# High and low weight parts interleaved element by element in one buffer of a two-layer encoder

## The chip, the cores and the metric

The kernel runs on one core of one Trainium2 chip. The metric is the device time of one execution in microseconds; a lower time is better. All times before come from two timed runs and one execution taken by the hardware profiler.

## The reference

A bidirectional encoder of two layers, 256 tokens, width 2048, all in float32:

```python
def reference(x, ...):
    for i in range(DEPTH):                      # DEPTH = 2
        h = rms_norm(x, attn_norm[i])
        if i % 2 == 0:
            x = x + even_mixer(h, ...)          # 16 heads: 8 neighbourhood, 8 dilated
        else:
            x = x + odd_mixer(h, ...)           # 16 query heads, 4 key/value heads, window 128
        x = x + sq_relu_mlp(rms_norm(x, mlp_norm[i]), w_mlp_in[i], w_mlp_out[i])
    return rms_norm(x, final_norm)

def sq_relu_mlp(h, w1, w2):                     # 2048 -> 8192 -> 2048
    a = jax.nn.relu(h @ w1)
    return (a * a) @ w2
```

Nearly all of the arithmetic is `activation @ weight`: projections into heads, the output projections, and the two large matrices of each MLP. Each weight is used once, for 256 tokens.

## The kernel before

**Precision.** A float32 product is put together from three products in the faster `float32r` format: a value is split into a high part (a copy rounded to `float32r`) and a low part (the value minus its high part), and high × high, high × low and low × high are added up. The activations `u`, `o`, `hid` hold both parts side by side, `[.., 2, 256]`. The weights arrive as plain float32 and are split on the chip, by the function `split(hi, lo, src)`: ScalarE (ACT) writes the high part as a copy (L82), VectorE (DVE) subtracts (L83).

**Tiling.** Weights come in units of 128 output features by 2048 inputs, and a unit in two halves of 8 tiles of 128 × 128 (`HALF = 8`), 512 KB each. `take_half` (from L96) takes the next half off a list written in the order of use, has SyncE (SP) load it into one of six buffers `r` (L100), and splits it into a tile `h` of the pool `whi` and a tile `l` of the pool `wlo`, five buffers each. Rows of these tiles are `ROW = P + 8 = 136` elements apart and 128 of them are used. The list runs two halves ahead of use. For every input tile k, `k_range` (L150 and L152) issues a pair of matmuls into one accumulator: `h` as the stationary operand against both parts of the activation (512 columns), then `l` against the high part (256 columns). In the tables a matmul is one row of PE and its load of the stationary tile one row of PEld.

**Exceptions.** Three things handle weights otherwise. `value_pair` (L272) takes weights as the moving operand and the activations as the stationary one; its halves are marked `flat` and lie without gaps, 1024 elements in a row. Where a unit must be held over a wait, its last two tiles are split into small tiles `hh` and `hl` of the pool `held_w`. And the first three units ("starters", L471 and L473) are loaded in groups of a few tiles together with the input, into tiles allocated at L461; the two halves of three units make six buffers, one more than a pool has.

**Order.** The program is written in the order of PE's use. Attention steps are put into that order some quarter units later (`later`, `tick`), and the framework's scheduler then orders the instructions of each engine by what they depend on and sets the waits. Every engine works its queue in order. A buffer of a pool is written anew when all readers of its last contents are done.

**Names.** `t` and `z` are the evacuation of an accumulator (`joined`, L179 and L181), `hid` the hidden layer's activation, `acc` an accumulator (three of them).

Of the kernel before, what the change touches and what calls it, by code (L numbers as in the profile page):

```python
# [8 lines left out]
F32R = mybir.dt.float32r  # L9
# [5 lines left out]
P = 128  # L15
# [9 lines left out]
SCALE = 128.0 ** -0.5  # L25
TW = 384
HALF = KT // 2
ROW = P + 8
RAW_BUFS = 6
PART_BUFS = 5  # L30

# [10 lines left out]
def encoder(ctx: ExitStack, tc: tile.TileContext, a: dict, outT: bass.AP):  # L42
# [1 line left out]

    const = ctx.enter_context(tc.tile_pool(name="const", bufs=1))
    raw = ctx.enter_context(tc.tile_pool(name="raw", bufs=RAW_BUFS))
    whi = ctx.enter_context(tc.tile_pool(name="whi", bufs=PART_BUFS))
    wlo = ctx.enter_context(tc.tile_pool(name="wlo", bufs=PART_BUFS))
    held_w = ctx.enter_context(tc.tile_pool(name="held_w", bufs=3))
    work = ctx.enter_context(tc.tile_pool(name="work", bufs=3))  # L50
    acc_ps = ctx.enter_context(tc.tile_pool(name="acc_ps", bufs=3, space=PSUM))
# [29 lines left out]
    def split(hi, lo, src):  # L81
        nc.scalar.activation(hi, src, AF.Copy)  # L82
        nc.vector.tensor_sub(lo, src, hi.bitcast(F32))  # L83
# [6 lines left out]
    def need(units, held=0, flat=False):  # L90

        for i, src in enumerate(units):
            pending.extend([(src[:, :HALF, :], HALF, flat),
                            (src[:, HALF:, :], HALF - 2 if i < held else HALF, flat)])

    def take_half():  # L96
        while pending and len(loaded) <= AHEAD:
            src, n, flat = pending.pop(0)
            r = raw.tile([P, HALF, P], F32, name="r")
            nc.sync.dma_start(r, src)  # L100
            h = whi.tile([P, HALF, ROW], F32R, name="h")
            l = wlo.tile([P, HALF, ROW], F32R, name="l")
            if flat:
                h, l = (w.rearrange("p k c -> p (k c)")[:, :HALF * P] for w in (h, l))
                split(h, l, r.rearrange("p k c -> p (k c)"))
                loaded.append((h, l, None))
                continue
            h, l = h[:, :, :P], l[:, :, :P]
            split(h[:, :n, :], l[:, :n, :], r[:, :n, :])
            tiles = [(h[:, k, :], l[:, k, :]) for k in range(n)]  # L110
            if n < HALF:
                h, l = (held_w.tile([P, 2, P], F32R, name=name) for name in ("hh", "hl"))
                split(h, l, r[:, n:, :])
                tiles += [(h[:, k, :], l[:, k, :]) for k in range(2)]
            loaded.append((h, l, tiles))
        return loaded.pop(0)

    def take_unit():
        return take_half()[2] + take_half()[2]
# [65 lines left out]
    def gained(k, which):  # L185
        x, gk = xs[:, k, :], g[:, which, k:k + 1]
        if which == 4:
            nc.scalar.activation(x, x, AF.Copy, scale=gk)
        else:
            nc.scalar.activation(u[:, k, 0, :], x, AF.Copy, scale=gk)  # L190
            nc.vector.scalar_tensor_tensor(u[:, k, 1, :], x, gk, u[:, k, 0, :].bitcast(F32),
                                           op0=ALU.mult, op1=ALU.subtract)
# [68 lines left out]
    def value_pair(pool, keep):  # L261

        ps = acc_ps.tile([P, 2, T], F32, name="acc")
        for half in range(2):
            parts = [take_half()[:2] for _ in range(2)]
            for kk in range(HALF):
                k = half * HALF + kk
                h, l = (w[:, (kk % 4) * T:(kk % 4 + 1) * T] for w in parts[kk // 4])
                for j in range(2):
                    js = slice(j * P, (j + 1) * P)  # L270
                    for n, (x, y) in enumerate(((0, h), (0, l), (1, h))):
                        nc.tensor.matmul(ps[:, j, :], u[:, k, x, js], y,  # L272
                                         start=k == 0 and j == 0 and n == 0,
                                         stop=k == KT - 1 and n == 2, skip_group_check=True)
                if kk % 2 == 1:
                    tick()
        assert norm["ready"]
        w = pool.tile([P, 2, 2, T], F32R, name="v", bufs=1)
        for j in range(2):
            nc.scalar.activation(w[:, 0, j, :], ps[:, j, :], AF.Copy, scale=rcol[:, j:j + 1])  # L280
            nc.vector.scalar_tensor_tensor(w[:, 1, j, :], ps[:, j, :], rcol[:, j:j + 1],
                                           w[:, 0, j, :].bitcast(F32), op0=ALU.mult, op1=ALU.subtract)
        keep.append(w)
# [158 lines left out]
    STARTERS = 3  # L442
# [14 lines left out]
    hl = [None] * STARTERS  # L457
    for k0, k1 in GROUPS:
        ks = slice(k0 % HALF, (k1 - 1) % HALF + 1)
        if k0 % HALF == 0:  # L460
            hl = [(whi.tile([P, HALF, ROW], F32R, name="h")[:, :, :P], wlo.tile([P, HALF, ROW], F32R, name="l")[:, :, :P])  # L461
                  for _ in range(STARTERS)]
        for i in range(STARTERS):
            split(hl[i][0][:, ks, :], hl[i][1][:, ks, :], rs[k0 // HALF][i][:, ks, :])
            if i == 0:
                for k in range(k0, k1):
                    gained(k, 0)
        for i in range(STARTERS):
            h, l = hl[i]
            for k in range(k0, k1):  # L470
                nc.tensor.matmul(sps[i], h[:, k % HALF, :], u[:, k].rearrange("p a t -> p (a t)"),  # L471
                                 start=k == 0, stop=False)
                nc.tensor.matmul(sps[i][:, :T], l[:, k % HALF, :], u[:, k, 0, :], start=False, stop=k == KT - 1)  # L473
# [12 lines left out]
    with tc.tile_pool(name="attn0", bufs=1) as pool:  # L486
# [24 lines left out]
        for p in range(8):  # L511
            q, k, v = [[], []], [[], []], []
            for i in range(2):
# [6 lines left out]
                h = 2 * p + i  # L520
# [11 lines left out]
    with tc.tile_pool(name="attn1", bufs=1) as pool:  # L532
        o = pool.tile([P, NH, 2, T], F32R, name="o")
        sl = slopes(16)
        for p in range(2):
            k, v = [[], []], []
# [8 lines left out]
            for i in range(8):  # L545
                h = 8 * p + i
# [93 lines left out]
```

## Time and profile before

| | |
|---|---|
| median of the timed runs | 2112.02 us (2111.78 to 2112.26, 2 runs) |
| the profiled execution | 2113.29 us, span 2111.4 us |
| PE busy | 2088.1 us, 12,438 matmuls |
| PEld busy | 1846.7 us, 12,438 loads |
| DVE busy | 1339.8 us |
| ACT busy | 1036.6 us |
| split, DVE's part (L83, tiles l) | 729 instructions, 880.6 us |
| split, ACT's part (L82, tiles h) | 729 instructions, 762.8 us |
| DMA | 386.06 MB, mean 183 GB/s |

The stages, in us from the span's start: start to 60; attention of layer 0 to 325; its output projection to 440; MLP of layer 0 to about 1125; then key, value and query projections of layer 1 with attention to 1300 (the table of the prediction cuts at 1195, shortly before the second group of eight heads); output projection to 1400; the second MLP to 2100. Busy times count instructions; matmuls overlap, so the time from one start to the next says how fast PE goes. A releaser is what ended an engine's idle time.

### The profile page before, as it was taken

What the parts mean: (1) busy time and instruction counts of PE and PEld (TensorE: products, weight loads), DVE (VectorE), ACT (ScalarE), POOL (GpSimd) and SP (SyncE); (2) the same over time, 40 slices, a digit from 0 to 9 for tenths busy, and PEclk for the clock granted to TensorE, in tenths of its full rate; (3) what the DMA queues carried; (4) which work ended last, traced back from release to release, by engine and by line L of the source; (5) the groups of instructions that cost most, each with busy time, mean ns of one, the idle gap of its engine ahead of it and who ended that gap; (6) DMA issues with size and microseconds to landing.
All of it is one profiled execution on the core that took longest, in us unless ns stands there. A gap on an engine that the chain in (4) does not pass through costs nothing.

```text
span 2111.4 us, 31825 instructions
## 1 busy us (share of the span) xinstructions
PE 2088.1 (99%) x12438; PEld 1846.7 (87%) x12438; DVE 1339.8 (63%) x2088; ACT 1036.6 (49%) x1602; POOL 23.0 (1%) x33
## 2 busy tenths in 40 slices
PE   8999999999999999999999999999999999999997
PEld 6999998888888888888889998888888888888887
DVE  6766676666655556666656877766665556665554
ACT  6555555544444444444445656554444434444442
POOL 2100000000000000000000000000000000000000
PEclk9999999999999999999999999999999999999999
DMA  9755555555555555555555454555555555555552
GB/s 260 176 174 167 168 174 174 191 185 189 189 188 189 189 189 189 190 189 190 189 189 185 149 163 144 190 185 188 189 189 189 189 189 189 189 189 190 189 189 91
DMA packets 108294, 386.06 MB, mean 183 GB/s; under 512 B 12352, under 2 KB 13392, under 8 KB 108144
## 3 DMA queue, kind: packets, MB, share of 16 engines
q1 hardware_dynamic: 106992, 381.73, 55.1%
q0 software_dynamic: 1008, 2.27, 1.5%
q8 instruction: 97, 1.59, 0.3%
q14 instruction: 53, 0.43, 0.1%
q10 hardware_dynamic: 144, 0.04, 0.0%
HBM read 381.89 MB, written 2.10 MB: 182 GB/s over the span
## 4 chain that ended last, share of the span: by engine, by line
PE 96%; DMA 2%; DVE 1%; ACT 0%; SPq 0%; issue 0%; DVEq 0%; ACTq 0%
PE acc L150 58%; PE acc L152 30%; PE acc L272 5%; PE s_ps L296 1%; PE m_ps L340 1%; DMA r<-in_even_w_in 1%; PE p_ps L321 1%; DMA r<-in_even_w_v 1%; DMA xs<-in_xT 0%; ACT h L82 0%; DVE l L83 0%; DVE xs L570 0%; PE acc L147 0%; PE acc L148 0%; PE m_ps L225 0%
## 5 line engine op out<-in xcount | busy, mean ns | idle before, releaser
L83 DVE TENSOR_TENSOR l<-r,h 128x1024 fp32r<-128x1024 f32 (+3 forms) x729 | 880.6, 1208 | 701.9 <-ACT h L82 699.3
L82 ACT ACTIVATE h<-r 128x1024 fp32r<-128x1024 f32 (+3 forms) x729 | 762.8, 1047 | 966.0 <-PE acc L150 635.9
L150 PE MATMUL acc<-u,h 128*128 128x512 f32 x2820 | 988.4, 394 | 0.0
L152 PE MATMUL acc<-u,l 128*128 128x256 f32 x2820 | 788.6, 280 | 0.0
L150 PE MATMUL acc<-hid,h 128*128 128x512 f32 x2016 | 702.4, 393 | 0.0
L150 PEld LDWEIGHTS acc<-u,h 128*128 128x128 f32 x2820 | 529.9, 188 | 119.2
L152 PE MATMUL acc<-hid,l 128*128 128x256 f32 x2048 | 572.3, 279 | 0.0
L152 PEld LDWEIGHTS acc<-u,l 128*128 128x128 f32 x2820 | 529.1, 188 | 0.2
L150 PEld LDWEIGHTS acc<-hid,h 128*128 128x128 f32 x2016 | 378.7, 188 | 87.3
L152 PEld LDWEIGHTS acc<-hid,l 128*128 128x128 f32 x2048 | 384.1, 188 | 0.0
L150 PE MATMUL acc<-o,h 128*128 128x512 f32 x500 | 175.2, 394 | 1.1 <-DVE z L181 1.1
L152 PE MATMUL acc<-o,l 128*128 128x256 f32 x500 | 139.8, 280 | 0.0
L272 PE MATMUL acc<-h,u 128*128 128x256 f32 x640 | 119.9, 283 | 0.0
L181 DVE TENSOR_TENSOR z<-acc,t 128x256 f32<-128x256 f32 x275 | 114.4, 418 | 2.2 <-ACT t L179 2.1
L150 PEld LDWEIGHTS acc<-o,h 128*128 128x128 f32 x500 | 93.9, 188 | 22.8 <-DVE z L181 1.7
L179 ACT ACTIVATE t<-acc 128x256 f32<-128x256 f32 x275 | 100.8, 367 | 5.5 <-PE acc L152 2.7
L272 PEld LDWEIGHTS acc<-h,u 128*128 128x128 f32 x640 | 101.1, 190 | 0.5
L152 PEld LDWEIGHTS acc<-o,l 128*128 128x128 f32 x500 | 93.8, 188 | 0.0
L272 PE MATMUL acc<-l,u 128*128 128x256 f32 x320 | 90.1, 281 | 0.0
L272 PEld LDWEIGHTS acc<-l,u 128*128 128x128 f32 x320 | 60.9, 190 | 0.1
L382 DVE SCALAR_TENSOR_TENSOR z<-z 128x256 f32<-128x256 f32 x128 | 54.2, 425 | 4.2
L83 DVE TENSOR_TENSOR hid<-z,hid 128x256 fp32r<-128x256 f32 x128 | 53.5, 419 | 1.3 <-ACT hid L82 1.2
(94 smaller groups left out, 857.6 us busy)
## 6 DMA issues: line engine op xcount, KB each, us to landing
r<-in_w_mlp_in SPq DMA_DIRECT2D x256, 512.0 KB, 4.5
r<-in_w_mlp_out SPq DMA_DIRECT2D x256, 512.0 KB, 4.5
r<-in_even_w_in SPq DMA_DIRECT2D x58, 512.0 KB, 4.2
r<-in_odd_w_qkv SPq DMA_DIRECT2D x40, 512.0 KB, 4.0
r<-in_even_w_v SPq DMA_DIRECT2D x32, 512.0 KB, 3.8
r<-in_even_w_out SPq DMA_DIRECT2D x32, 512.0 KB, 4.2
r<-in_odd_w_out SPq DMA_DIRECT2D x32, 512.0 KB, 3.8
r<-in_odd_w_v SPq DMA_DIRECT2D x8, 512.0 KB, 4.1
```

Source lines behind the costliest of these rows:

```text
L82: nc.scalar.activation(hi, src, AF.Copy)
L83: nc.vector.tensor_sub(lo, src, hi.bitcast(F32))
L150: nc.tensor.matmul(ps, h, act[:, k].rearrange("p a t -> p (a t)"), start=start, stop=False)
L152: nc.tensor.matmul(ps[:, :T], l, act[:, k, 0, :], start=False, stop=stop)
L179: nc.scalar.activation(t, ps[:, T:], AF.Copy)
L181: nc.vector.tensor_add(z, ps[:, :T], t)
L272: nc.tensor.matmul(ps[:, j, :], u[:, k, x, js], y, start=k == 0 and j == 0 and n == 0, stop=k == KT - 1 and n == 2, skip_group_check=True)
L296: nc.tensor.matmul(s_ps[:, i, :], qh[:, x, qs], kh[:, y, :], start=n == 0, stop=n == 2)
L321: nc.tensor.transpose(p_ps[:, j, i * P:(i + 1) * P], s[:, i, j * P:(j + 1) * P], ident)
L340: nc.tensor.matmul(o_ps[:, :T], vv[:, x, j, side * P:(side + 1) * P], pt[:, y, j, :], start=n == 0, stop=n == 5)
L382: nc.vector.scalar_tensor_tensor(z, z, 0.0, z, op0=ALU.max, op1=ALU.mult)
```

## The change

The pools `whi` and `wlo` become one pool `parts_w` of five buffers whose rows are `2 * P + 8 = 264` elements apart. High parts lie in the elements 0, 2, 4, ... of a row and low parts in 1, 3, 5, .... ACT therefore writes every other element, DVE reads the high part and writes the low part with the same step, and each load of a stationary tile reads 128 elements at a step of two elements (8 bytes). The small held tiles are interleaved in the same way. The halves of `value_pair` are not: there the high part fills the first 1024 elements and the low part the next 1024. The number and shapes of the instructions stay the same.

```diff
-ROW = P + 8
+ROW = 2 * P + 8
...
-    whi = ctx.enter_context(tc.tile_pool(name="whi", bufs=PART_BUFS))
-    wlo = ctx.enter_context(tc.tile_pool(name="wlo", bufs=PART_BUFS))
+    parts_w = ctx.enter_context(tc.tile_pool(name="parts_w", bufs=PART_BUFS))
...
+    def interleaved(w):
+        return w[:, :, 0:2 * P:2], w[:, :, 1:2 * P:2]
+
     def take_half():
         while pending and len(loaded) <= AHEAD:
             src, n, flat = pending.pop(0)
             r = raw.tile([P, HALF, P], F32, name="r")
             nc.sync.dma_start(r, src)
-            h = whi.tile([P, HALF, ROW], F32R, name="h")
-            l = wlo.tile([P, HALF, ROW], F32R, name="l")
+            w = parts_w.tile([P, HALF, ROW], F32R, name="w")
             if flat:
-                h, l = (w.rearrange("p k c -> p (k c)")[:, :HALF * P] for w in (h, l))
+                w = w.rearrange("p k c -> p (k c)")
+                h, l = w[:, :HALF * P], w[:, HALF * P:2 * HALF * P]
                 split(h, l, r.rearrange("p k c -> p (k c)"))
                 loaded.append((h, l, None))
                 continue
-            h, l = h[:, :, :P], l[:, :, :P]
+            h, l = interleaved(w)
             split(h[:, :n, :], l[:, :n, :], r[:, :n, :])
             tiles = [(h[:, k, :], l[:, k, :]) for k in range(n)]
             if n < HALF:
-                h, l = (held_w.tile([P, 2, P], F32R, name=name) for name in ("hh", "hl"))
+                h, l = interleaved(held_w.tile([P, 2, 2 * P], F32R, name="hw"))
                 split(h, l, r[:, n:, :])
...
         if k0 % HALF == 0:
-            hl = [(whi.tile([P, HALF, ROW], F32R, name="h")[:, :, :P], wlo.tile([P, HALF, ROW], F32R, name="l")[:, :, :P])
-                  for _ in range(STARTERS)]
+            hl = [interleaved(parts_w.tile([P, HALF, ROW], F32R, name="w")) for _ in range(STARTERS)]
```

On PE the order is the same but for a few attention steps, which stand up to ten places earlier or later among the pairs. On ACT and DVE neighbours change places. What moves are waits. The first place is the start, at the sixth starter buffer, the one that no pool has free; ACT's queue before:

```order
L82 ACTIVATE h<-r 128x4x128 [waits DMAHW6_49]
L190 ACTIVATE u<-xs,g 128x256 x2
L82 ACTIVATE h<-r 128x4x128 [waits DMAHW7_49]
L82 ACTIVATE h<-r 128x4x128 [waits DMAHW0_49,PE_49]
L199 ACTIVATE sq<-xs 128x256 [waits DVE_49]
```

The same place of ACT's queue in the changed kernel, where w is the shared tile:

```order
L81 ACTIVATE w<-r 128x4x128 [waits DMAHW6_49]
L192 ACTIVATE u<-xs,g 128x256 x2
L81 ACTIVATE w<-r 128x4x128 [waits DMAHW7_49]
L81 ACTIVATE w<-r 128x4x128 [waits DMAHW0_49,DVE_49,PE_49]
L201 ACTIVATE sq<-xs 128x256 [waits DVE_49]
```

The copy into the sixth buffer now waits for DVE as well, which wrote the low part there, and its wait for PE covers the low part's matmuls too. DVE's queue at the same place, before:

```order
L83 TENSOR_TENSOR l<-r,h 128x4x128 [waits DMAHW6_49,Activation_49]
L191 SCALAR_TENSOR_TENSOR u<-xs,g,u 128x256 [waits Activation_49] x2
L83 TENSOR_TENSOR l<-r,h 128x4x128 [waits DMAHW7_49,Activation_49]
L83 TENSOR_TENSOR l<-r,h 128x4x128 [waits DMAHW0_49,PE_49,Activation_49]
L200 TENSOR_TENSOR ssq<-ssq,sq 128x256 [waits DVE_49,Activation_49]
```

And in the changed kernel:

```order
L82 TENSOR_TENSOR w<-r,w 128x4x128 [waits DMAHW6_49,Activation_49]
L193 SCALAR_TENSOR_TENSOR u<-xs,g,u 128x256 [waits Activation_49] x2
L82 TENSOR_TENSOR w<-r,w 128x4x128 [waits DMAHW7_49,Activation_49]
L82 TENSOR_TENSOR w<-r,w 128x4x128 [waits DMAHW0_49,Activation_49]
L202 TENSOR_TENSOR ssq<-ssq,sq 128x256 [waits DVE_49,Activation_49]
```

DVE's subtraction has lost its wait for PE; it waits for ACT's copy, which has waited for PE. The second place is ACT's queue in the middle of the first MLP's hidden units, before (h a high part, t an evacuation, hid the hidden activation):

```order
L82 ACTIVATE h<-r 128x8x128 [waits DMAHW5_49,PE_49,Activation_49]
L179 ACTIVATE t<-acc 128x256 [waits PE_49,Activation_49]
L82 ACTIVATE h<-r 128x8x128 [waits DMAHW6_49,PE_49]
L82 ACTIVATE hid<-z 128x256 [waits DVE_49]
L82 ACTIVATE h<-r 128x8x128 [waits DMAHW7_49,PE_49,Activation_49]
L179 ACTIVATE t<-acc 128x256 [waits PE_49,Activation_49]
```

And in the changed kernel:

```order
L81 ACTIVATE w<-r 128x8x128 [waits DMAHW0_49,PE_49,Activation_49]
L181 ACTIVATE t<-acc 128x256 [waits PE_49,Activation_49]
L81 ACTIVATE w<-r 128x8x128 [waits DMAHW1_49]
L81 ACTIVATE hid<-z 128x256 [waits DVE_49]
L81 ACTIVATE w<-r 128x8x128 [waits DMAHW2_49,PE_49,Activation_49]
L181 ACTIVATE t<-acc 128x256 [waits PE_49,Activation_49]
```

The order of kinds is the same. Every second copy has no wait for PE of its own any more: its buffer comes free with the last low-part matmul of a unit, for which the evacuation ahead of it has already waited.

## The prediction

> **What bounds the kernel now.** First the page's busy shares, the granted clock and the chain that ended last.
>
> ```profile
> PE 2088.1 (99%) x12438; PEld 1846.7 (87%) x12438; DVE 1339.8 (63%) x2088; ACT 1036.6 (49%) x1602; POOL 23.0 (1%) x33
> ...
> PEclk9999999999999999999999999999999999999999
> ...
> PE 96%; DMA 2%; DVE 1%; ACT 0%; SPq 0%; issue 0%; DVEq 0%; ACTq 0%
> ```
>
> TensorE is busy 99% of the span and makes 96% of the chain. So only two things can move the time: the cadence of the matmuls, or another engine that becomes late enough to stop them. The cadence is read from the timeline of a moment deep in the first MLP.
>
> ```profile
> 1004.56 0.40 PE L150 MATMUL acc<-hid,h 128*128 128x512 f32 x1
> 1004.56 0.19 PEld L152 LDWEIGHTS acc<-hid,l 128*128 128x128 f32 x1
> 1004.80 0.28 PE L152 MATMUL acc<-hid,l 128*128 128x256 f32 x1
> 1004.80 0.19 PEld L150 LDWEIGHTS acc<-hid,h 128*128 128x128 f32 x1
> 1004.91 0.40 PE L150 MATMUL acc<-hid,h 128*128 128x512 f32 x1
> 1004.92 0.19 PEld L152 LDWEIGHTS acc<-hid,l 128*128 128x128 f32 x1
> 1005.15 0.28 PE L152 MATMUL acc<-hid,l 128*128 128x256 f32 x1
> 1005.15 0.19 PEld L150 LDWEIGHTS acc<-hid,h 128*128 128x128 f32 x1
> ```
>
> Starts matter here, not durations, since the instructions overlap. A high-part matmul (512 columns) holds PE from 1004.56 to 1004.80 and a low-part matmul (256 columns) from 1004.80 to 1004.91; the pair comes round every 0.35 us. Each matmul has a weight load of its own, issued when the matmul before it starts. The low part's load has a slot of 0.23 to 0.24 us, the next high part's load only 0.11 to 0.12 us. The load takes 0.19 us from start to end, longer than the short slot, so successive loads overlap, and what is exclusive in a load is shorter than its duration. The groups by shape give the number of pairs, and the chain gives the two slots and a stretch in which every matmul has 256 columns and a load.
>
> ```profile
> L150 PE MATMUL acc<-u,h 128*128 128x512 f32 x2820 | 988.4, 394 | 0.0
> ...
> L150 PE MATMUL acc<-hid,h 128*128 128x512 f32 x2016 | 702.4, 393 | 0.0
> L150 PEld LDWEIGHTS acc<-u,h 128*128 128x128 f32 x2820 | 529.9, 188 | 119.2
> ...
> L150 PE MATMUL acc<-o,h 128*128 128x512 f32 x500 | 175.2, 394 | 1.1 <-DVE z L181 1.1
> ```
> ```profile
> 122.06 0.23 PE acc L150
> 122.28 0.12 PE acc L152
> 122.40 1.42 PE acc L272 x12
> ...
> 124.26 5.66 PE acc L272 x48
> ```
>
> That is 2820 + 2016 + 500 = 5,336 pairs, about 0.348 us each: 1,857 of the 2,111 us. The value projections (L272) run at 5.66 / 48 = 0.118 us a matmul.
>
> **The change part by part.** Base: the profiled execution took 2113.3 us, its span 2111.4 and 1.9 around it; the median of the runs is 2112.0, so the sum is made as a difference and put on the median.
>
> *Matmuls and loads.* None is added or removed; both halves of a pair now load their stationary tile with a step of 8 bytes, 1,024 bytes of a partition instead of 512. The trace of before has no such load. From below: 0, because a load is no limit as long as its exclusive part fits the short slot of 0.117 us. From above: if that part fills the slot already and goes with the bytes it spans, the short slot becomes 0.234 us, and 5,336 × 0.117 = +624 us. I take 0. The row it is nearest to is the moving operand's: the high-part matmul reads 512 contiguous elements, 2,048 bytes of each partition, in 0.23 us, so 1,024 bytes take half of that, 0.115 us. A load that touches 1,024 bytes at that rate still fits 0.117 us, though barely. A value below 0 is weighed with the rivals.
>
> The Trainium skill ("TensorE: Matmul & The Clock Gate", LDWEIGHTS) speaks against this comfort: it gives a load as its columns over 1.2 per ns, an estimate of 107 ns for 128, which would leave 10 ns of the slot. By it any slowing of a load by over a tenth shows, and a doubling costs an estimated 97 ns a pair, +518 us in all. The 117 ns slots do not contradict it.
>
> *Splits.* ACT's copy now writes every other element; DVE reads h and writes l that way.
>
> ```profile
> L83 DVE TENSOR_TENSOR l<-r,h 128x1024 fp32r<-128x1024 f32 x702 | 860.6, 1226 | 688.7 <-ACT h L82 686.2
> L82 ACT ACTIVATE h<-r 128x1024 fp32r<-128x1024 f32 x702 | 744.9, 1061 | 946.6 <-PE acc L150 625.2 <-issue 289.5 <-PE acc L272 11.8
> ...
> L83 DVE TENSOR_TENSOR l<-r,h 128x256 fp32r<-128x256 f32 x6 | 2.5, 424 | 5.8 <-ACT h L82 5.8
> ...
> L82 ACT ACTIVATE h<-r 128x256 fp32r<-128x256 f32 x6 | 2.5, 410 | 5.5 <-DMA r<-in_even_w_in 5.5
> ```
>
> Per element DVE costs (1226 − 424) / 768 = 1.044 ns and ACT (1061 − 410) / 768 = 0.848 ns. No row has a stepped access of these engines, so the bounds are: nothing, and a doubling of the part per element (twice the bytes spanned). That part is 1,069 of DVE's 1,226 ns (87%) and 868 of ACT's 1,061 (82%). Whether PE would feel it is read by stage, all work first and then only the instructions that read the raw tiles, the splits:
>
> ```profile
> 325.00:440.00 115.00, 114.51 (x659) 100.14 (x659) 78.56 (x126) 63.71 (x104) 0.00 (x0) 1.00 0.56 183
> 440.00:1195.00 755.00, 755.00 (x4390) 663.40 (x4389) 467.06 (x668) 355.62 (x508) 0.00 (x0) 1.00 0.57 187
> 1195.00:1300.00 105.00, 104.91 (x694) 95.54 (x693) 82.58 (x206) 63.37 (x138) 0.00 (x0) 1.00 0.46 152
> 1300.00:1400.00 100.00, 99.44 (x575) 87.02 (x574) 69.78 (x111) 57.02 (x94) 0.00 (x0) 1.00 0.56 184
> 1400.00:2085.00 685.00, 685.00 (x3933) 599.79 (x3933) 409.10 (x540) 316.70 (x429) 0.00 (x0) 1.00 0.57 185
> ```
> ```profile
> 325.00:440.00 115.00, 49.52 (x45) 43.16 (x44) 1.00 0.56 183
> 440.00:1195.00 755.00, 329.04 (x273) 284.61 (x271) 1.00 0.57 187
> 1195.00:1300.00 105.00, 36.91 (x33) 32.62 (x34) 1.00 0.46 152
> 1300.00:1400.00 100.00, 43.49 (x39) 37.50 (x38) 1.00 0.56 184
> 1400.00:2085.00 685.00, 300.46 (x248) 261.24 (x246) 1.00 0.57 185
> ```
>
> Columns: in the first table PE, PEld, DVE, ACT, POOL after the length; in the second DVE and ACT. DVE idles 36.4, 287.9, 22.4, 30.2 and 275.9 us in these stages. A doubling adds 87% of the second table: 43.2, 286.9, 32.2, 37.9 and 262.0. It overflows by 6.8, 9.8 and 7.7 us in the first, third and fourth stage and just fits in the two MLP stretches: +24 us. ACT always fits (tightest: 63.4 + 0.82 × 32.6 = 90 of 105 us). So the splits are priced 0 to +24 us; I take 0, because the rows of these engines show times per element, no times per byte.
>
> *Waits.* As the order shows, ACT's copy now waits for the last low-part matmul on the old buffer, and DVE's subtraction no longer waits for PE.
>
> ```profile
> DVE l L83 <- ACT h L82: 699.3, 659, 4.1
> ACT h L82 <- PE acc L150: 635.9, 432, 2.0
> ...
> PEld acc L471 <- ACT h L82: 7.7, 5, 2.2
> ```
>
> The first two rows say that splits are run as soon as a buffer comes free. With five buffers, a freed one is read again four halves later, 4 × 8 × 0.348 = 11.1 us; copy and subtraction take 1.06 + 1.23 = 2.3 us of that. The release comes later by one low-part slot, 0.12 us (0.35 us where the next high part lies between), and behind the waiting copy on ACT stand the evacuation t and the hidden layer's copy; the three accumulators cover those. Without that cover it would be at most 0.35 us a half. Where it bites is the start, the only place where PE's loads waited for splits for long (third row): the sixth starter buffer, +0.4 us at most. If the splits doubled, the start would lose some 3 us, five waits of a 512-element split that is 0.43 to 0.53 us longer. The swaps of neighbours on ACT and DVE cost nothing by the same 11.1 us.
>
> Sum: 2112.0 + 0 + 0 + 0.4 = **2112.4 us**.
>
> **The rivals.** *Slower: the stepped load becomes the bound* (the other side). Place: the short slot. It decides from the point where a load's exclusive part exceeds 0.117 us. In full it gives 2112 + 624 = 2736 us. In part, say 5 to 25 ns over the slot, 5,336 × 5 to 25 ns = +27 to +133 us, 2139 to 2245. For it: there is no more than one short slot for each pair, PE has nothing to hide a longer load behind, and the byte argument leaves 2 ns. Against: the rate of the moving stream.
>
> *DVE becomes the bound.* Up to a doubling 2112 to 2139 us; over 2% slower only from 2.05 times the time per element, where the two MLP stretches overflow as well (at that factor 8.9 + 13.4 + 11.4 + 9.6 = 43 us). At 2.4 times, where I end this case, the same table overflows by 24 + 114 + 23 + 23 + 91 = 275 us: 2387.
> The Trainium skill's "Vector Engine (DVE) Microarchitecture Reference" (5.2, measured stream behaviour) has a rule for this: a port keeps its rate only for runs of two adjacent 4-byte words, which a step of two never gives; its rows run from 1.71 to 2.50 ns a column, and by my stage table that is nothing at 1.75 and an estimated +270 us at 2.50. "SBUF — State Buffer" (its cacheline note) says two hits on a 16-byte line suffice, which a step of 8 bytes gives: nothing. No run here shows either yet.
>
> *Faster: the pair gets shorter.* At half the granted clock (the column after POOL in the second fence) a pair took 0.64 us:
>
> ```profile
> 21.20 0.41 PE L473 MATMUL acc<-u,l 128*128 128x256 f32 x1
> 21.41 0.63 PE L471 MATMUL acc<-u,h 128*128 128x512 f32 x1
> 21.84 0.41 PE L473 MATMUL acc<-u,l 128*128 128x256 f32 x1
> ```
> ```profile
> 21.00:22.50 1.50, 1.50 (x6) 1.21 (x6) 1.50 (x5) 1.23 (x4) 0.00 (x0) 0.50 0.77 78
> ```
>
> Half of that is 0.320, so 0.028 us a pair is lost at full clock. If the stationary reads from two buffers caused it and one buffer removed it, 5,336 × 0.028 = −149 us, 1963 us. Against: L272, whose stationary tile lies in u, loses as much (0.118 where half the clock's 0.21 gives 0.107).
>
> That the step would not reach PE is excluded: in the order both matmuls of a pair take the one tile w, with unchanged shapes.
>
> **How the numbers follow.** Nothing shows: 0.57 (2108 to 2117). DVE slower, mostly hidden: 0.17 (2112 to 2139). DVE beyond 2.05 times: 0.05 (2155 to 2387). Load in part over the slot: 0.05 (2139 to 2245). Load in full: 0.11 (2630 to 2736). Faster: 0.05 (1963 to 2070). No change within 2%, which is about what can be told from none here, is the first two cases, 0.74, less 0.01 for a combination of both engines: 0.73; slower 0.22, faster 0.05. The range runs from 2104 to 2250 us: the first two cases, the partly longer load and half of the DVE tail, 0.81.
>
> **What would show it.** Right: pairs still every 0.348 us, DVE's split near 1,226 ns, ACT's near 1,061, waits of PE for splits only in the first 60 us. A longer load shows as a longer low-part slot (0.12 us in the chain) with the high-part slot unchanged, and a longer PEld mean than 188 ns. A slow DVE shows as a split mean over 2 us and PE waiting for w in the stages after 325 and 1195 us. The prediction is wrong if a memory path counts accesses and not bytes.

## The result, and the profile after

The changed kernel takes **2130.7 us** (2129.6 to 2131.9, two runs) against 2112.0: ratio 1.0082, 95% interval 1.0061 to 1.0104. It is 18.7 us slower, less than the 2% under which a change counts as none here, but clear of the noise. The profiled execution took 2129.55 us, its span 2127.6, 16.2 more than before. The busy shares and the chain's first line of the page:

```profile
PE 2103.1 (99%) x12438; PEld 1896.6 (89%) x12438; DVE 1358.4 (64%) x2088; ACT 1108.4 (52%) x1602; POOL 21.8 (1%) x33
...
PEclk9999999999999999999999999999999999999999
...
PE 96%; DMA 1%; DVE 1%; SPq 1%; issue 0%; ACT 0%; DVEq 0%; ACTq 0%
```

PE's busy time grew by 15.0 us (2088.1 to 2103.1) with the same 12,438 matmuls at the same granted clock, and its idle time (span less busy) only from 23.3 to 24.5. So the time did not go into waits; the matmuls come more slowly. The groups by shape:

```profile
L82 DVE TENSOR_TENSOR w<-r,w 128x1024 fp32r<-128x1024 f32 x702 | 860.4, 1226 | 498.9 <-ACT w L81 478.7
L81 ACT ACTIVATE w<-r 128x1024 fp32r<-128x1024 f32 x702 | 803.5, 1145 | 482.0 <-PE acc L154 427.3 <-PE acc L274 27.0 <-issue 17.4
...
L154 PEld LDWEIGHTS acc<-u,w 128*128 128x128 f32 x2820 | 552.0, 196 | 0.2
L152 PEld LDWEIGHTS acc<-u,w 128*128 128x128 f32 x2820 | 549.6, 195 | 101.0
```

The low parts' loads before, beside the row of the high parts' that the prediction shows:

```profile
L152 PEld LDWEIGHTS acc<-u,l 128*128 128x128 f32 x2820 | 529.1, 188 | 0.2
```

The loads went from 188 to 195 and 196 ns, ACT's copy from 1061 to 1145, DVE's subtraction stayed at 1226. What a pair costs is read from a stretch of the first MLP that holds nothing but pairs, 560 us long: the number of matmuls in it, after PE's busy time, tells the cadence. Before, and then after:

```profile
440.00:1000.00 560.00, 560.00 (x3217) 490.31 (x3216) 338.64 (x449) 256.29 (x351) 0.00 (x0) 1.00 0.58 189
```
```profile
440.00:1000.00 560.00, 560.00 (x3195) 501.57 (x3194) 341.82 (x445) 274.54 (x346) 0.00 (x0) 1.00 0.57 188
```

2 × 560 / 3217 = 348.2 ns a pair before, 2 × 560 / 3195 = 350.5 after: 2.4 ns more. (The count takes in the matmuls that reach over the two edges, so both figures are some 0.2 ns low, and all others made this way below.) Over the 5,336 pairs of the prediction that is 12.8 of the 16.2 us. From the starts of all matmuls after the first 70 us, without those slots that other work stretches beyond 300 ns, the long slot grew from 230.9 to 232.6 ns and the short one from 117.6 to 118.4.

### The profile page after: what moved, and what is told of

The parts are those of the page before. It is cut to its first block, busy times and chain, and to the rows that moved or that the text cites. A ratio compares the mean times of both kernels' runs of the same rounds, so it can differ in the third digit from the quotient of the medians.

```text
span 2127.6 us, 31836 instructions
## 1 busy us (share of the span) xinstructions
PE 2103.1 (99%) x12438; PEld 1896.6 (89%) x12438; DVE 1358.4 (64%) x2088; ACT 1108.4 (52%) x1602; POOL 21.8 (1%) x33
## 4 chain that ended last, share of the span: by engine, by line
PE 96%; DMA 1%; DVE 1%; SPq 1%; issue 0%; ACT 0%; DVEq 0%; ACTq 0%
PE acc L152 58%; PE acc L154 30%; PE acc L274 5%; PE m_ps L342 1%; PE s_ps L298 1%; PE p_ps L323 1%; DMA r<-in_even_w_in 1%; DMA r<-in_even_w_v 0%; SPq L453 0%; DVE w L82 0%; ACT w L81 0%; DVE xs L571 0%; PE acc L150 0%; PE acc L149 0%; DMA g<-in_gains 0%
## 5 line engine op out<-in xcount | busy, mean ns | idle before, releaser
L82 DVE TENSOR_TENSOR w<-r,w 128x1024 fp32r<-128x1024 f32 (+3 forms) x729 | 880.5, 1208 | 512.0 <-ACT w L81 491.6
L81 ACT ACTIVATE w<-r 128x1024 fp32r<-128x1024 f32 (+3 forms) x729 | 822.8, 1129 | 497.9 <-PE acc L154 433.8
L152 PE MATMUL acc<-u,w 128*128 128x512 f32 x2820 | 995.2, 395 | 0.0
L154 PE MATMUL acc<-u,w 128*128 128x256 f32 x2820 | 794.3, 282 | 0.0
L152 PE MATMUL acc<-hid,w 128*128 128x512 f32 x2016 | 707.5, 394 | 0.0
L152 PEld LDWEIGHTS acc<-u,w 128*128 128x128 f32 x2820 | 549.6, 195 | 101.0
L154 PE MATMUL acc<-hid,w 128*128 128x256 f32 x2048 | 576.9, 282 | 0.0
L154 PEld LDWEIGHTS acc<-u,w 128*128 128x128 f32 x2820 | 552.0, 196 | 0.2
L152 PEld LDWEIGHTS acc<-hid,w 128*128 128x128 f32 x2016 | 392.7, 195 | 73.8
L154 PEld LDWEIGHTS acc<-hid,w 128*128 128x128 f32 x2048 | 400.6, 196 | 0.0
L152 PE MATMUL acc<-o,w 128*128 128x512 f32 x500 | 176.5, 395 | 1.5 <-DVE z L183 1.5
L152 PEld LDWEIGHTS acc<-o,w 128*128 128x128 f32 x500 | 97.4, 195 | 20.0 <-DVE z L183 2.1
L154 PEld LDWEIGHTS acc<-o,w 128*128 128x128 f32 x500 | 97.8, 196 | 0.0
```

The source lines that it names most:

```text
L152: nc.tensor.matmul(ps, h, act[:, k].rearrange("p a t -> p (a t)"), start=start, stop=False)
L154: nc.tensor.matmul(ps[:, :T], l, act[:, k, 0, :], start=False, stop=stop)
```

## The experiments

Three theories were set against each other. A: a load that reads with a step of two slows the pair. B: the shared buffer, the distance of its rows, or its waits do. C: the stepped accesses of ACT and DVE disturb PE's reads. In every run the kernel before ran on the same chip and took 2112.0 to 2113.4 us.

**1. One buffer without a step.**

```diff
     def interleaved(w):
-        return w[:, :, 0:2 * P:2], w[:, :, 1:2 * P:2]
+        return w[:, :, :P], w[:, :, P:2 * P]
```

> The changed kernel with its one pool, its row pitch of 264 elements and its waits, but the high part in the first 128 elements of a row and the low part in the next 128: no step anywhere. Theory A (reading the stationary tile with a step of two slows the pair of matmuls, 348.5 ns before, 351.0 after): 2111 to 2114 us, pair 348.5 ns, load 188 ns, ACT's copy 1061 ns. Theory C (the stepped writes of ACT and DVE disturb PE's reads): the same, 2111 to 2114. Theory B (the shared buffer, its pitch or its waits): 2128 to 2132 us, pair 351 ns.

Measured: 2114.5 us, ratio 1.0012 (1.0003 to 1.0021). The same groups, of this run, and its stretch:

```profile
L82 DVE TENSOR_TENSOR w<-r,w 128x1024 fp32r<-128x1024 f32 x702 | 860.0, 1225 | 465.7 <-ACT w L81 452.0
L81 ACT ACTIVATE w<-r 128x1024 fp32r<-128x1024 f32 x702 | 742.4, 1058 | 492.1 <-PE acc L154 440.4 <-PE acc L274 23.9 <-issue 16.8
```
```profile
440.00:1000.00 560.00, 560.00 (x3217) 490.33 (x3216) 344.15 (x450) 263.33 (x349) 0.00 (x0) 1.00 0.57 189
```

3217 matmuls again, and ACT's copy is back at 1058 ns. Theory B falls: pool, row distance and waits are those of the changed kernel, and together they are worth 2.5 us (0.6 to 4.4 by the interval). The other 16 us came with the step. One thing moved along with it: the low part starts at element 128 of its row here and at element 1 in the changed kernel, while the high part starts at the same place in both.

**2. The kernel before, with splits that step.** The splits walk the even elements, then the odd ones; the loads stay contiguous.

```diff
+    def by_two(w):
+        return w.rearrange("p k (c s) -> p k s c", s=2)
+
+    def split_stepped(hi, lo, src):
+        split(by_two(hi), by_two(lo), by_two(src))
...
-            split(h[:, :n, :], l[:, :n, :], r[:, :n, :])
+            split_stepped(h[:, :n, :], l[:, :n, :], r[:, :n, :])
```

> The kernel before, with two pools and contiguous loads, but both parts of a split walk through their tile in steps of two elements (first the even elements, then the odd ones), in reading and writing. The values stored are the same. Theory A and B: 2111 to 2114 us, pair 348.5 ns. Theory C: 2126 to 2131 us, pair 351 ns with the load's mean still 188 ns. On ACT alone: if the step in its writes is why its copy went from 1061 to 1150 ns, 1140 to 1160 here too; if it is the low parts that lie between, 1061.

Measured: 2114.6 us, ratio 1.001 (1.0001 to 1.0019). Groups and stretch:

```profile
L83 DVE TENSOR_TENSOR l<-r,h 128x1024 fp32r<-128x1024 f32 x702 | 862.0, 1228 | 689.9 <-ACT h L82 688.3
L82 ACT ACTIVATE h<-r 128x1024 fp32r<-128x1024 f32 x702 | 800.8, 1141 | 898.8 <-PE acc L156 595.1 <-issue 259.6 <-ACT sq L205 13.5
```
```profile
440.00:1000.00 560.00, 560.00 (x3217) 490.36 (x3216) 338.70 (x449) 271.76 (x351) 0.00 (x0) 1.00 0.58 189
```

ACT's copy is slow in the same way, 1141 ns, and the cadence is untouched. Theory C falls. The run also shows that ACT's 80 ns are the price of a stepped access, and that the whole edit costs 2.6 us (0.2 to 4.0 by the interval) while ACT has room; DVE, at 1228 ns, pays none in reading or writing. Run 1 differs from before by as much without a step, so what these 2 to 3 us are was not found.

**3 and 4. A stepped load by itself.** For a step in the loads alone, two weight tiles lie side by side in one row, and a stationary tile takes every other column out of both; the control (`STEP_H, STEP_L = 1, 1`) reads them one after the other. The products of the stepped kernel are therefore of mixed weights; only its time is used, and that of runs 5, 6 and 8 likewise. The tiles become `[P, HALF // G, ROW]`, the splits stay contiguous, and all else is the kernel before.

```diff
-ROW = P + 8
+G = 2
+ROW = G * P + 8
+STEP_H, STEP_L = 2, 2
...
+    def load(w, k, step, n):
+        if step == 1 or n < G:
+            return w[:, k // G, k % G * P:(k % G + 1) * P]
+        return w[:, k // G, k % G:G * P:G]
```

> Control for the next run. The kernel before, with two neighbouring tiles k side by side in one row of 264 elements (no gap between the two), loads contiguous. Theory A and C: 2110 to 2114 us. If the distance between tiles matters (part of B), it differs from 2112 by more than 3 us.

> As the control, two pools, contiguous splits, the same waits; only the loads differ: a stationary tile takes its 128 columns with a step of two out of the 256 of a pair, so that its columns come in turn from two weight tiles and the products are those of mixed weights. Theory A: 13 to 19 us over the control, pair 351 ns, load 195 ns, and ACT's copy 1061 ns. Theory B and C: within 3 us of the control.

Measured: the control 2122.9 us (ratio 1.0047, 1.0034 to 1.0059), the stepped one 2133.1 (1.0095, 1.0082 to 1.0109). Their stretches, control first:

```profile
440.00:1000.00 560.00, 560.00 (x3200) 488.92 (x3199) 335.79 (x446) 254.53 (x347) 0.00 (x0) 1.00 0.58 188
```
```profile
440.00:1000.00 560.00, 560.00 (x3184) 500.31 (x3183) 334.95 (x444) 253.25 (x346) 0.00 (x0) 1.00 0.57 187
```

350.0 and 351.8 ns a pair. The step adds 10.2 us here, less than the 13 to 19 us that theory A expected. The loads and the copy of the stepped run:

```profile
L84 ACT ACTIVATE h<-r 128x1024 fp32r<-128x1024 f32 x702 | 744.4, 1060 | 966.6 <-PE acc L170 641.0 <-issue 292.3 <-PE acc L292 14.3
L172 PEld LDWEIGHTS acc<-u,l 128*128 128x128 f32 x2820 | 552.3, 196 | 0.2
L170 PEld LDWEIGHTS acc<-u,h 128*128 128x128 f32 x2820 | 550.0, 195 | 102.7
```

Theory A holds in kind. But the control itself is 11 us slower than before though it steps nowhere: the place of the tiles matters, which the expectation had named only as a possible part of theory B, and which run 1 did not show.

The step also moves the start of every second tile of a row (from its element 128 to its element 1). The traces can tell the two apart, tile by tile, from the starts of about 1,000 pairs of each kind where the MLPs read `hid`: pairs of the tiles that keep their start went from 350.2 to 354.7 ns, pairs of those that moved from 350.8 to 350.0. So the 10 us are not the price of the moved starts, as far as one pair can be told from its neighbours.

**5 and 6. Which load it is.** The kernel of run 4 with a step for the high parts alone, then for the low parts alone (run 6 has `1, 2` in this line).

```diff
-STEP_H, STEP_L = 2, 2
+STEP_H, STEP_L = 2, 1
```

> Only the high parts' loads take a step of two (their columns come in turn from two weight tiles, so the products are mixed); the low parts' loads are contiguous. Control without a step: 2122.9 us, pair 350.2 ns (long slot 232.5, short 117.7); both with a step: 2133.1 us, pair 352.1 (234.4 and 117.7). The load of the high part is issued in the short slot and ends after the next high-part matmul has begun. Theory H (the longer high-part load holds up the beginning of the matmul that uses it, so the long slot grows): about 2133 us, long slot 234.4. Theory L (a stepped load in the long slot disturbs the reads of the matmul that runs there): 2122 to 2124 us, long slot 232.5.

> The counterpart: only the low parts' loads take a step of two, the high parts' are contiguous. Theory H: 2122 to 2124 us, long slot 232.5, with the low loads at 195 ns and the high loads at 188. Theory L: about 2133 us, long slot 234.4. If both share the cost: 2127 to 2129 us in both runs.

Measured: high alone 2130.5 us (ratio 1.0088, 1.0073 to 1.0103), low alone 2120.7 (1.0041, 1.0026 to 1.0056). High alone:

```profile
L170 PEld LDWEIGHTS acc<-u,h 128*128 128x128 f32 x2820 | 551.0, 195 | 120.0
L172 PEld LDWEIGHTS acc<-u,l 128*128 128x128 f32 x2820 | 532.9, 189 | 0.2
...
440.00:1000.00 560.00, 560.00 (x3187) 490.32 (x3186) 334.98 (x444) 253.64 (x347) 0.00 (x0) 1.00 0.55 187
```

Low alone:

```profile
L172 PEld LDWEIGHTS acc<-u,l 128*128 128x128 f32 x2820 | 552.1, 196 | 0.2 <-DVE l L85 0.2
L170 PEld LDWEIGHTS acc<-u,h 128*128 128x128 f32 x2820 | 530.2, 188 | 101.2
...
440.00:1000.00 560.00, 560.00 (x3204) 501.63 (x3203) 336.55 (x447) 254.71 (x347) 0.00 (x0) 1.00 0.55 188
```

The stepped load is 7 to 8 ns longer in either place, but only the high part's is paid for: +7.6 us over the control, against −2.3 for the low part's, whose slot is twice as long (the intervals of run 6 and the control overlap, so that is no gain). That is theory H's side, the load that has only the short slot to run in. The sizes don't add up (7.6 − 2.3 = 5.3, both together 10.2), though with intervals of some 3 us either way on each run this may be noise. The mechanism of H came only in part: the long slot grew to 233.3 ns where H expected 234.4, and the short one grew as well, from 117.6 to 118.4.

**7 and 8. A step of four.** Four tiles side by side; the loads contiguous (the control, `1, 1`), and then every fourth element, 16 bytes apart. The edit is shown against run 4.

```diff
-G = 2
-STEP_H, STEP_L = 2, 2
+G = 4
+STEP_H, STEP_L = 4, 4
```

> Control for the next run: four neighbouring tiles side by side in a row of 520 elements, two pools, contiguous loads. If the place of the tiles matters as in the control of pairs (2122.9 us against 2112.0): between 2108 and 2126 us. If only the gap of 8 elements after each tile were at fault there: 2123 to 2130 us, since there are fewer gaps here.

> Loads take a step of four elements, 16 bytes: the 128 columns of a stationary tile come in turn from four weight tiles, so the products are mixed. Theory of bytes spanned (a step of two adds 7.5 ns to a load and 1.9 ns to a pair for 512 bytes more; a step of four spans 1,536 more): load 208 to 212 ns, pair 5 to 8 ns over the control, 25 to 45 us over it. Rival with a cliff (a load is slowed in earnest only when no two of its elements lie within 16 bytes): load over 240 ns, the short slot over 150 ns, 200 us or more over the control. Rival without size (any step costs the same): load 195 ns, 10 us over the control.

Measured: the control 2114.0 us (ratio 1.0009, 1.0000 to 1.0019), the step of four **2769.1** (1.3114, 1.3094 to 1.3133). From the latter's timeline:

```profile
1299.96 0.28 PE L172 MATMUL acc<-hid,l 128*128 128x256 f32 x1
1299.97 0.31 PEld L170 LDWEIGHTS acc<-hid,h 128*128 128x128 f32 x1
...
1300.08 0.51 PE L170 MATMUL acc<-hid,h 128*128 128x512 f32 x1
...
1300.18 0.33 PEld L172 LDWEIGHTS acc<-hid,l 128*128 128x128 f32 x1
1300.43 0.29 PE L172 MATMUL acc<-hid,l 128*128 128x256 f32 x1
```

The theory of bytes spanned, which expected 25 to 45 us, falls by more than a factor of ten: the cost jumps between 8 and 16 bytes. Whether there is an edge at 16 bytes or a gradual rise is not shown. At the rate of the moving stream that the prediction used (0.115 us for 1,024 bytes), a load that spans 2,048 bytes would take 0.23 us, near what is found below, and a step of three was not run. The rows show how a load becomes the bound: the high part's load begins at 1299.97, and the low part's only at 1300.18, 0.21 us later, though the matmul before it began at 1300.08. Until then (rows of before) a load began within 0.01 us of that matmul. So one load now seems to hold the path for at least 0.21 us, and the two of a pair no longer fit under the 0.348 us that a pair took: it takes 0.47 us (1299.96 to 1300.43). The rival that foresaw a cliff had it in the short slot; it is the long one that grew, to 0.35 us, since the low part's load stands in line behind the high part's.

**9 to 12. The place of the tiles.** The distance of rows alone, contiguous and interleaved.

Run 9, against the kernel before (run 10 has `P + 4`):

```diff
-ROW = P + 8
+ROW = P
```

Run 11, against the changed kernel (run 12 has `2 * P + 16`):

```diff
-ROW = 2 * P + 8
+ROW = 2 * P
```

> The kernel before with rows of 128 elements: no gap between tiles, so all tiles of a buffer start at a multiple of 512 bytes. The controls so far went from 2112 us (gap of 8 after each tile) and 2114 (after each fourth) to 2123 (after each second), with everything contiguous. Theory P (the place of a tile within its buffer sets the slots): another time than 2112, between 2106 and 2125 us, with the slots of the eight tiles alike, since all tiles start alike. Rival (the gap does not matter, pairs was slow for another reason): 2111 to 2114.

> The kernel before with rows of 132 elements, the mean distance of the control of pairs (2122.9 us, pair 350.2 ns), but evenly spaced. Theory P: not 2112; if the distance of 132 is what counts, 2120 to 2125 us. Rival: 2111 to 2114.

> The changed kernel with rows of 256 elements: interleaved, step of two, no gap between tiles. Theory S (a step of two costs a pair 1.9 to 2.5 ns wherever the tiles lie): 10 to 19 us over the run without a gap and without a step. Theory P alone (the step costs by the place it happened to get): anything from equal to the run without a gap to 30 us over it.

> The changed kernel with rows of 272 elements instead of 264. Theory S: 2126 to 2136 us, load 195 ns. Theory P alone: it can come back to 2112 to 2118 us with the load still at 195 ns.

Measured, with the pair from the stretch of 560 us (the ratios of runs 9 to 12 are to the 2113.4 us of before beside them):

| run | step of the loads | row | us | ratio (95%) | matmuls in 560 us | pair, ns |
|---|---|---|---|---|---|---|
| before | 1 | 128 + 8 | 2112.0 | | 3217 | 348.2 |
| 10 | 1 | 128 + 4 | 2122.9 | 1.0050 (1.0033 to 1.0067) | 3201 | 349.9 |
| 9 | 1 | 128 | 2129.1 | 1.0075 (1.0060 to 1.0090) | 3183 | 351.9 |
| after | 2 | 256 + 8 | 2130.7 | 1.0082 (1.0061 to 1.0104) | 3195 | 350.5 |
| 11 | 2 | 256 | 2132.1 | 1.0090 (1.0072 to 1.0108) | 3186 | 351.5 |
| 12 | 2 | 256 + 16 | 2139.8 | 1.0127 (1.0112 to 1.0142) | 3171 | 353.2 |

```profile
440.00:1000.00 560.00, 560.00 (x3183) 487.09 (x3182) 334.99 (x444) 252.83 (x346) 0.00 (x0) 1.00 0.55 187
```
```profile
440.00:1000.00 560.00, 560.00 (x3186) 500.80 (x3185) 339.84 (x442) 271.37 (x346) 0.00 (x0) 1.00 0.53 187
```

These are runs 9 and 11. The loads of run 11:

```profile
L152 PEld LDWEIGHTS acc<-u,w 128*128 128x128 f32 x2820 | 553.2, 196 | 101.7
L154 PEld LDWEIGHTS acc<-u,w 128*128 128x128 f32 x2820 | 552.3, 196 | 0.2
```

Without a gap the contiguous kernel is as slow as the interleaved one: on the mean the step costs a pair nothing there, though its loads are 196 ns long, and the two runs are 3.0 us apart with intervals that overlap. Theory S, a fixed price of the step on top of the run without a gap, expected 10 to 19 us and falls in that form. The two runs are no clean pair, though: tiles start 512 bytes apart in run 9 and 1,024 in run 11, so a price of the step that a better place offsets is not excluded.

Theory P holds in kind: place alone moves a pair from 348.2 to 351.9 ns without any step. Its sizes did not come: run 9 lies above its 2106 to 2125 us, and run 12, at 2139.8 us, above what either theory expected. With a step of two in both loads a pair was never below 350.5 in the four placements tried. Where the MLPs read `hid`, the starts of the matmuls in run 9 repeat every two tiles (long slots of 233 and 230 ns in turn) and not every one, as P expected; in run 11 all eight are alike (232.5 ns); before, they repeat every eight (226 to 237 ns). In all three the pattern is the same in every buffer.

None of the runs beats the kernel before.

## Why the prediction was right or wrong

**The bound** was read rightly: PE's cadence, with no other engine near enough to stop it. 15.0 of the 16.2 us are PE's busy time.

**Loads.** This is the term that was mis-sized: 0 taken, 2.4 ns a pair measured, 12.8 us, and with them the predicted 2112.4 came out 18.3 us low, inside the range. That the number lies inside is partly luck. It is outside the case that the forecast rested on (2108 to 2117) and below the partly longer load (2139 to 2245), the rival nearest to what happened; it falls into the band of a slower DVE, which did not happen. The bounds of 0 and +624 us held, and the mechanism of the partly longer load was named as a rival, at 27 us and more. Of the signs of being right two failed, the pair at 0.348 us and ACT's copy near 1,061 ns, and one sign of a longer load came, a PEld mean above 188 ns. The argument from the moving stream's rate got the large thing right, that a load of 1,024 bytes still just fits, and run 8 shows loads that no longer fit at +655 us. What it missed is that a load within its slot still costs something. It was also wrong on where this would show: the long slot took 1.7 of the added nanoseconds and the short one 0.8, where a longer short slot with an unchanged long one had been named as the sign.

The Trainium skill ("TensorE: Matmul & The Clock Gate", LDWEIGHTS) gives a load as its columns over 1.2 per ns, an estimate of 107 ns for 128; that it leaves little room agrees with the 0.21 us of run 8, twice that figure for a step of four. The Trainium skill's "SBUF — State Buffer" (cachelines) puts the edge where two reads no longer fall into one line of 16 bytes, and the jump between the steps of two and four agrees. Since 2,048 bytes at the moving stream's rate give nearly the same, no run here decides between the two.

**Splits.** DVE's share was priced right, 0: 1226 ns as before. The Trainium skill's "Vector Engine (DVE) Microarchitecture Reference" (5.2) asks for adjacent pairs of words at full rate; at a step of two DVE kept 1226 ns, so the rule as stated did not hold for this subtraction, and the rival built on it is out. (Of that rival's working, one reading is off: at 2.05 times, the four overflows that it adds up hold only the first of the two MLP stretches.) For ACT the row of before was followed where it could not tell: 8% on the copy, hidden by the room that the stage table gave it, as run 2 shows.

**Waits.** +0.4 us were allowed; PE's idle time grew by 1.2 us (23.3 to 24.5). Run 1 puts pool, distance and waits together at 2.5 us (0.6 to 4.4 by its interval). Where those lie was not found: the cadence of that run is unchanged.

**The faster rival** went the wrong way, but its thought had something: 0.028 us a pair is lost at full clock, and part of that does hang on where the stationary tiles lie. One buffer did not win it back (run 1: 3217 matmuls in 560 us, as before).

**What stays open.** Why the place of a tile changes the slots, and why the step's price goes from 2.4 ns (against run 1) over 1.8 (runs 3 and 4) to nothing (runs 9 and 11). No two runs differ in the step alone with every tile's start held; the tile by tile reading of run 4 is the nearest to that. That the load of the high part, with its short slot, carries the cost was shown in one placement only. So the 16 us of the step can be put down to stepped loads *in this placement*, not to a fixed price of a step.

## What to carry to other kernels

Where PE sets the time, count what each matmul's weight load has beside it: its slot is the matmul before it, and a load that fits by a few nanoseconds is no free load. A step of two float32 elements in the stationary operand cost under 1%, a step of four 31%; so on this evidence two things may be interleaved if the layout asks for it, and four may not where PE sets the time. Before a layout is judged by its step, run the same rows without the step: here the place of the tiles alone was worth nearly as much as the whole change (0.75% in run 9, 0.82% for the change).

## What the runs showed that was not expected

- A gap of 8 elements after each stationary tile makes a pair 3.7 ns shorter than none (348.2 against 351.9), about 16 us of the kernel (run 9 against the before beside it), with nothing else changed; gaps after every second tile give 350.0, after every fourth 348.3 (3216 matmuls in 560 us).
- A step of two in its writes slows ACT's copy by 8% (1061 to 1145 ns); the same step in DVE's reads and writes costs nothing (1226 and 1228 ns).
- With a step of four, loads are no longer hidden: the share of PEld goes to 99%.

```profile
PE 2748.1 (99%) x12438; PEld 2739.3 (99%) x12438; DVE 1343.6 (49%) x2100; ACT 1038.8 (38%) x1614; POOL 24.3 (1%) x33
```
